# Part-of-12 stages of the second MLP projection: four seven-product blocks at 0, 3, 6, 8 instead of three at 0, 4, 8

## The chip, the cores and the metric

The kernel runs on one core of a Trainium2 chip. The metric is the device time of one execution in microseconds (us). The core has a matrix engine (TensorE, PE in the rows; its weight loads are PEld), a vector engine (VectorE, DVE), a scalar engine (ScalarE, ACT), GpSimd (POOL) and a sync engine (SyncE, SP) that here only issues loads from device memory.

## What is computed

One decoder layer on 256 tokens of width 2048: three mixing branches, and behind them a squared-ReLU MLP. The change touches the last product of the MLP alone:

```
h2 = rmsnorm(x, norm2_g[l])
x = x + jnp.square(jax.nn.relu(h2 @ w_mlp_in[l])) @ w_mlp_out[l]
return rmsnorm(x, final_g)
```

`w_mlp_out` is 8192 x 2048 in float32. The kernel keeps float32 accuracy by splitting every operand into a high part `hi` (rounded to the matrix engine's fast float32 format) and a remainder `lo`, and by running three matmuls, hi·hi, lo·hi and hi·lo, for each product.

## The kernel before

**Parts.** The 8192 hidden columns are done in three parts of 12, 12 and 8 blocks of 256 (`PARTS`). For each part the kernel first computes the hidden activations (stage m1, `do_m1`, `run_W`), then multiplies them with the matching rows of `w_mlp_out` in two halves `h` of 1024 output columns (stage m2s, `do_m2s`, `run_seven`), and adds the result to `x2`. The last half of the last part goes another way (`do_m2`).

**Blocks.** A block is 256 rows of the weight by 1024 output columns, for 256 tokens. Done in the standard way it is 2 x 2 x 2 half-block products (two halves each of tokens, rows and columns), each of three matmuls of 128 x 128 by 512 columns: 24 matmuls. A seven-product block gets the same result from 7 products of sums and differences (a scheme of Strassen's kind): 21 matmuls. Before, blocks 0, 4, 8 of the parts of 12 and 0, 4 of the part of 8 are done so: 3 + 3 + 3 + 3 + 2 = 14.

**Units.** The weight comes in units of 512 KB. A standard block is two units (below: 9a is the first unit of block 9, 9b the second). For each, SP loads `raw` (line 218), ACT rounds it to `hi` and DVE forms `lo` = raw - hi (both in `conv_to`). A seven-product block has three units, a, c and e, of which e has no load: `conv_seven` makes `d` = raw(a) - raw(c) on DVE, splits `d` for unit c, and builds the sums of unit e in the second raw buffer, in place, from `d` and both raw buffers, so that both stay taken until unit e is nearly done:

```
            V.tensor_add(x[:, 0, :], d[:, 1, :], a[:, 0, :])
            V.tensor_sub(x[:, 1, :], x[:, 1, :], x[:, 0, :])
            loaded[u] = (*split_unit(u, x), b)
```

The chain of a seven-product block is therefore serial: hi and lo of a, `d`, hi and lo of `d`, `b` (ACT and DVE), two in-place steps on the second raw, hi and lo of it.

**Buffers and order.** There are four `raw` buffers (`NRAW`), used in turn, and five each for `hi` and `lo`. Every engine runs its instructions in the order in which the code issues them; `begin_unit(u, 3)` issues the loads up to unit u + 5 and the conversions up to unit u + 3, then what `later` has put off (evacuations), then the matmuls of unit u. A load waits on SP until its raw buffer is free, that is until the unit four loads earlier has been converted.

**Accumulators.** `run_seven` holds all eight PSUM banks: `top` and `bot` (two banks each, the two token halves) and four side banks `p1`, `p5`, `p6`, `p7` for products that several outputs share. The side banks are read two slots after the last seven-product block (`ev_shared`, four DVE additions behind two ACT copies), `top` and `bot` at the end (`ev`, DVE instructions `m2r<-top`, `m2r<-bot`). The next stage's `top` takes the same two banks. In the code `m2r<-top` is issued inside the last unit, behind the conversions up to three units ahead: in the first half of a part that is behind a, c and e of the next stage's block 0.

**Forms.** The sums of activations that a seven-product block needs are made once per part in stage m1 (`sums`: four DVE additions, an ACT rounding and a DVE subtraction) and kept in a tile of their own for both halves.

Of the kernel before, what the change touches and what calls it, by code (L numbers as in the profile page):

```python
# [17 lines left out]
P = 128  # L18
# [18 lines left out]
PARTS = (12, 12, 8)  # L37
FIRST = [sum(PARTS[:q]) for q in range(len(PARTS) + 1)]
LAST = len(PARTS) - 1
EVERY = 4  # L40


C_G1, C_G2, C_GM, C_D, C_GLU = 0, 16, 32, 40, 48
# [53 lines left out]
def hybrid_trunk(  # L97
# [37 lines left out]
    def a4(shape, dt, name):  # L135
        return acts.tile(shape, dt, tag="a4", name=name)
# [13 lines left out]
    units, seven = [], {}  # L150

    def add_units(src, g, k0, k1):
        r = []
        for ku in range(k0, k1):
            r.append(len(units))
            units.append(src[g, ku])
        return r
# [22 lines left out]
    for q, nk in enumerate(PARTS):  # L180
        for i in range(0, nk, 2):
            g = FIRST[q] + i
            if (q, i) == (0, 0):
                ab = [add_units(w_m1, 0, 0, 3), add_units(w_m1, 1, 0, 3)]
                for j in range(2):
                    ab[j] += add_units(w_m1, j, 3, 4)
                plan.append(("m1", (q, i), ab))
            else:
                plan.append(("m1", (q, i), [add_units(w_m1, g + j, 0, 4) for j in range(2)]))
        for h in range(2):  # L190
            if (q, h) == (LAST, 1):
                for c in (2, 3):
                    plan.append(("m2", (q, c), add_units(w_m2, c, FIRST[q], FIRST[q + 1])))
                continue
            us = []
            for k in range(nk):
                ku = FIRST[q] + k
                if k % EVERY == 0:
                    n = len(units)
                    units.extend((w_seven[h, ku // EVERY, 0], w_seven[h, ku // EVERY, 1], None))  # L200
                    seven.update({n: "a", n + 1: "c", n + 2: "e"})
                    us.append((n, n + 1, n + 2))
                else:
                    us.append([add_units(w_m2, 2 * h + c, ku, ku + 1)[0] for c in range(2)])
            plan.append(("m2s", (q, h), us))
# [107 lines left out]
    def later(n, f):  # L313
        late.append((slot[0] + n, f))
# [14 lines left out]
    def run_W(groups, src, at_once=False):  # L329

        steps = [(g, i) for g, (us, _) in enumerate(groups) for i in range(len(us) - 1)]
        steps += [(g, len(us) - 1) for g, (us, _) in enumerate(groups)]
        pts = {}
        for g, i in steps:
            us, evac = groups[g]
            if g not in pts:
                pts[g] = two_banks(f"mm{us[0]}")
            pt = pts[g]  # L340
            last = 4 * len(us) - 1
            hi, lo = (w.rearrange("p a (b c) -> p (a b) c", b=2) for w in begin_unit(us[i], 3))
            for nb in range(2):
                for k in range(4):
                    PE.matmul(pt[:, nb, :], lhsT=hi[:, k, nb * P:(nb + 1) * P], rhs=src.both(4 * i + k),  # L345
                              start=4 * i + k == 0, stop=False)
            for nb in range(2):
                for k in range(4):
                    PE.matmul(pt[:, nb, T:], lhsT=lo[:, k, nb * P:(nb + 1) * P], rhs=src.hi(4 * i + k),  # L349
                              start=False, stop=4 * i + k == last)  # L350
            if i == len(us) - 1:
                if at_once:
                    evac(pt)
                else:
                    later(1, lambda pt=pt, evac=evac: evac(pt))
            end_unit()

    def wide_sum(ps, name):

        t = t2k([P, 2, T], name)  # L360
        S.copy(t, ps[:, :, T:])  # L361
        V.tensor_add(t, ps[:, :, :T], t)
        return t
# [169 lines left out]
    def split2(dst, i, src):  # L533

        t = dst.pair(i)
        S.copy(t[:, :, 0, :], src)
        V.tensor_sub(t[:, :, 1, :], src, t[:, :, 0, :].bitcast(F32))
# [679 lines left out]
    def do_m1(q, i0, uss):  # L1217
        if i0 == 0:
            ffs[q] = Split(env, 2 * PARTS[q], f"ff{q}_")
            forms[q] = {}  # L1220

        def ev(ps, i):
            t = wide_sum(ps, f"relu{q}_{i}")

            def square():
                V.scalar_tensor_tensor(out=t, in0=t, scalar=0.0, in1=t, op0=ALU.max, op1=ALU.mult)
                split2(ffs[q], i, t)
                if i % EVERY == 0:
                    later(1, sums)

            def sums():

                f = s5w.tile([P, 4, P], F32, tag="gb", name=f"sums{q}_{i}", bufs=1)
                V.scalar_tensor_tensor(out=f[:, 0, :], in0=t[:, 0, P:], scalar=-1.0, in1=t[:, 1, P:],
                                       op0=ALU.mult, op1=ALU.subtract)
                V.scalar_tensor_tensor(out=f[:, 1, :], in0=f[:, 0, :], scalar=-1.0, in1=t[:, 0, :P],
                                       op0=ALU.mult, op1=ALU.subtract)
                V.tensor_sub(f[:, 2, :], t[:, 0, :P], t[:, 0, P:])
                V.tensor_sub(f[:, 3, :], t[:, 1, :P], f[:, 1, :])
                fs = forms[q][i] = a4([P, 4, 2, P], F32R, f"form{q}_{i}")  # L1240
                S.copy(fs[:, :, 0, :], f)
                V.tensor_sub(fs[:, :, 1, :], f, fs[:, :, 0, :].bitcast(F32))

            later(1, square)

        groups = [(us, lambda ps, i=i0 + j: ev(ps, i)) for j, us in enumerate(uss)]
        if (q, i0) == (0, 0):
            run_W(groups, xs2)
        else:
            for j, g in enumerate(groups):  # L1250
                run_W([g], xs2, at_once=i0 + j == PARTS[q] - 1)
# [96 lines left out]
def _tiles(w):  # L1348

    k, n = w.shape  # L1350
    return np.ascontiguousarray(w.reshape(k // 256, 2, P, n // 512, 512).transpose(3, 0, 2, 1, 4))
# [9 lines left out]
def _cols(v):  # L1361
    return v.reshape(-1, P).T


def _layout(x, norm1_g, w_in, b_gate, gm_norm_g, gm_w_s, gm_b_s, s5_lambda_re, s5_lambda_im, s5_log_dt,
            s5_b_re, s5_b_im, s5_c_re, s5_c_im, s5_d, s5_w_glu, s5_b_glu, w_branch, w_out, norm2_g,
            w_mlp_in, w_mlp_out, final_g):
    a = {}
    a["x"] = x.reshape(T, D)
    a["xT"] = x.reshape(T, 4, 4, P).transpose(1, 3, 2, 0)  # L1370
    a["w_in"] = _tiles(w_in[0])
    a["w_wide"] = _tiles_T(np.concatenate([w_in[0][:, c:c + MIX] for c in (0, 3 * MIX, 4 * MIX)], axis=1))
    a["w_br"] = np.stack([_tiles(w_branch[0, n]) for n in range(3)])
    a["w_out"] = _tiles(w_out[0])
    a["w_glu"] = _tiles(s5_w_glu[0])
    a["w_m1"] = _tiles_T(w_mlp_in[0])
    a["w_m2"] = _tiles(w_mlp_out[0])

    b = a["w_m2"].reshape(2, 2, -1, P, 2, 512)[:, :, ::EVERY]
    a["w_seven"] = np.stack([np.stack([b[:, r, :, :, 0], b[:, 1 - r, :, :, 1]], axis=3) for r in range(2)],  # L1380
                            axis=2)
    a["cols"] = np.concatenate([_cols(norm1_g[0]), _cols(norm2_g[0]), _cols(gm_norm_g[0]),
                                _cols(s5_d[0]), _cols(s5_b_glu[0])], axis=1)
    a["b_gate"] = b_gate[0]
    a["final_g"] = final_g
    a["gm_ws"] = gm_w_s[0].transpose(2, 0, 1)
    a["gm_bs"] = gm_b_s[0]

    def states(v):
        return v.reshape(NPAIR, P).T  # L1390

    par = np.empty((P, 3, NPAIR), np.float32)
    par[:, 0] = states(s5_lambda_re[0])
    par[:, 1] = states(s5_lambda_im[0])
    par[:, 2] = states(np.broadcast_to(s5_log_dt[0][:, None], (64, 64)))
    a["s5_par"] = par
    b = np.zeros((4, 2, 16, 8, 2, 2, 64), np.float32)
    c = np.zeros((2, 64, 8, 2, 4, 2, 16), np.float32)
    for ri, (bb, cc) in enumerate(((s5_b_re, s5_c_re), (s5_b_im, s5_c_im))):
        bb = bb[0].reshape(8, 4, 2, 64, 16)  # L1400
        cc = cc[0].reshape(8, 4, 2, 16, 64)
        for r in range(2):
            b[:, r, :, :, ri, r, :] = bb[:, :, r].transpose(1, 3, 0, 2)
            c[r, :, :, ri, :, r, :] = cc[:, :, r].transpose(3, 0, 1, 2)
    a["s5_b"] = b.reshape(P, 8, 2 * P)
    a["s5_c"] = c.reshape(P, 8, 2, 4, 32)
    return {n: np.ascontiguousarray(v) for n, v in a.items()}
# [15 lines left out]
```

## Time and profile before

| | |
|---|---|
| median of 3 runs | 1533.29 us (1532.86 to 1533.46) |
| the profiled execution | 1534.34 us |
| its span on the core | 1532.4 us |
| PE busy | 1521.0 us, 99% |
| DVE busy | 1183.3 us, 77% |
| ACT busy | 783.2 us, 51% |
| the four m2s stages of the parts of 12 | 63.38, 63.36, 63.38 and 63.36 us |

The page gives the busy time of each engine over the span, the chain of work that ended last, and the costliest groups of instructions. A matmul's row shows about 0.39 us although the next one starts 0.23 us later, since they are pipelined; so stages are read by starts, not by busy time. Instructions of DVE and ACT start up to 0.1 us before the row of the one ahead of them ends.

### The profile page before, as it was taken

Reading aid. Unit: us, or ns where it says so; the run is one execution under the profiler, and the core shown is the slowest. Engines: PE = TensorE matmul, PEld = TensorE weight load, DVE = VectorE, ACT = ScalarE, POOL = GpSimd, SP = SyncE. Lnnn points to the kernel's source line nnn. Section 1 sums busy time; section 2 is a strip of 40 time slices with the busy share of each in tenths; the row PEclk is TensorE's granted clock in tenths of the full one; section 3 lists DMA queues with packets and bytes.
Section 4 is the critical chain, followed back from the end, with each engine's and each line's share of the span. In section 5 each row is a group of like instructions: output and inputs, shape, how many; then the busy total and the mean of one; then the engine's idle time right before and its main releaser. Section 6 shows DMA issues by size and latency. Waiting matters only on the chain.

```text
span 1532.4 us, 20783 instructions
## 1 busy us (share of the span) xinstructions
PE 1521.0 (99%) x7906; PEld 1291.8 (84%) x7906; DVE 1183.3 (77%) x1588; ACT 783.2 (51%) x994; POOL 12.2 (1%) x21
## 2 busy tenths in 40 slices
PE   9999999999999999999999999999999999999997
PEld 9988888887887887898888888888888888888886
DVE  6996988999998999967655666786766678776675
ACT  7445768455555554555445444545444454544452
POOL 0000000000000000000000000000000000000000
PEclk9999999999999999999999999999999999999999
DMA  9664555555555656555665555656556466655554
GB/s 353 210 195 140 183 191 164 184 189 193 191 199 187 203 188 220 180 185 189 214 222 180 188 185 163 219 185 212 196 192 193 154 207 202 222 191 186 198 179 151
DMA packets 85507, 298.18 MB, mean 195 GB/s; under 512 B 9632, under 2 KB 10656, under 8 KB 85408
## 3 DMA queue, kind: packets, MB, share of 16 engines
q1 hardware_dynamic: 79200, 285.25, 56.2%
q10 hardware_dynamic: 6208, 11.61, 2.4%
q8 instruction: 62, 1.02, 0.3%
q14 instruction: 37, 0.30, 0.1%
HBM read 294.73 MB, written 2.10 MB: 194 GB/s over the span
## 4 chain that ended last, share of the span: by engine, by line
PE 95%; DVE 2%; DMA 1%; ACT 1%; issue 1%; SPq 0%; POOLq 0%; POOL 0%; DVEq 0%; ACTq 0%
PE mm L345 20%; PE mm L410 13%; PE mm L411 13%; PE mm L413 13%; PE mm L349 10%; PE top L436 9%; PE bot L436 8%; PE p L436 3%; PE mm L379 1%; PE mm L387 1%; PE mm L380 1%; DMA raw<-in_w_m 1%; DVE lo L91 1%; PE pb L779 1%; PE py L879 1%
## 5 line engine op out<-in xcount | busy, mean ns | idle before, releaser
L91 DVE TENSOR_TENSOR lo<-raw,hi 128x1024 fp32r<-128x1024 f32 (+1 forms) x537 | 645.8, 1219 | 169.9 <-ACT hi L241 142.9
L241 ACT CAST hi<-raw 128x1024 fp32r<-128x1024 f32 (+1 forms) x509 | 526.1, 1049 | 285.8 <-PE mm L411 113.7
L345 PE MATMUL mm<-xz,hi 128*128 128x512 f32 x1024 | 256.5, 392 | 0.0
L345 PEld LDWEIGHTS mm<-xz,hi 128*128 128x128 f32 x1024 | 184.3, 189 | 33.1
L410 PE MATMUL mm<-hi,xs 128*128 128x512 f32 x512 | 201.4, 393 | 0.0
L411 PE MATMUL mm<-hi,xs 128*128 128x512 f32 x512 | 199.6, 390 | 0.0
L349 PEld LDWEIGHTS mm<-xz,lo 128*128 128x128 f32 x1024 | 139.7, 190 | 10.0
L349 PE MATMUL mm<-xz,lo 128*128 128x256 f32 x1024 | 142.8, 282 | 0.0
L413 PE MATMUL mm<-lo,xs 128*128 128x512 f32 x512 | 136.9, 389 | 0.0
L410 PEld LDWEIGHTS mm<-hi,xs 128*128 128x128 f32 x512 | 96.1, 188 | 23.5 <-issue 4.1
L413 PEld LDWEIGHTS mm<-lo,xs 128*128 128x128 f32 x512 | 96.1, 188 | 20.2
L411 PEld LDWEIGHTS mm<-hi,xs 128*128 128x128 f32 x512 | 96.2, 188 | 19.4
L436 PE MATMUL bot<-hi,ff 128*128 128x512 f32 x364 | 98.6, 389 | 0.0
L345 PE MATMUL mm<-xs,hi 128*128 128x512 f32 x384 | 96.9, 394 | 0.0
L436 PE MATMUL top<-hi,ff 128*128 128x512 f32 x336 | 89.8, 389 | 0.0
L345 PEld LDWEIGHTS mm<-xs,hi 128*128 128x128 f32 x384 | 69.1, 189 | 13.6 <-issue 0.7
L436 PEld LDWEIGHTS bot<-hi,ff 128*128 128x128 f32 x364 | 68.3, 188 | 14.3
L91 DVE TENSOR_TENSOR rt<-bu,cs 128x1024 f32<-128x1024 f32 x64 | 76.5, 1218 | 0.3
L436 PEld LDWEIGHTS top<-hi,ff 128*128 128x128 f32 x336 | 63.1, 188 | 13.2
L436 PE MATMUL bot<-lo,ff 128*128 128x512 f32 x182 | 57.2, 389 | 0.0
L91 DVE TENSOR_TENSOR relu<-mm,relu 128x512 f32<-128x512 f32 x32 | 22.1, 690 | 44.6 <-ACT relu L361 44.6
L349 PEld LDWEIGHTS mm<-xs,lo 128*128 128x128 f32 x384 | 52.4, 190 | 3.8
(292 smaller groups left out, 2056.5 us busy)
## 6 DMA issues: line engine op xcount, KB each, us to landing
raw<-in_w_m SPq DMA_DIRECT2D x228, 512.0 KB, 4.3
raw<-in_w_in SPq DMA_DIRECT2D x143, 512.0 KB, 4.1
raw<-in_w_wide SPq DMA_DIRECT2D x48, 512.0 KB, 3.9
raw<-in_w_br SPq DMA_DIRECT2D x48, 512.0 KB, 4.4
raw<-in_w_out SPq DMA_DIRECT2D x32, 512.0 KB, 4.3
raw<-in_w_seven SPq DMA_DIRECT2D x28, 512.0 KB, 4.6
x<-in_x ACTq DMA_DIRECT2D x8, 512.0 KB, 6.5
raw<-in_w_glu SPq DMA_DIRECT2D x8, 512.0 KB, 4.5
```

The source lines that it names most:

```text
L91: return fn(*a, **kw)
L241: S.copy(hi[:, k, :], raw[:, k, :])
L345: PE.matmul(pt[:, nb, :], lhsT=hi[:, k, nb * P:(nb + 1) * P], rhs=src.both(4 * i + k), start=4 * i + k == 0, stop=False)
L349: PE.matmul(pt[:, nb, T:], lhsT=lo[:, k, nb * P:(nb + 1) * P], rhs=src.hi(4 * i + k), start=False, stop=4 * i + k == last)
L379: PE.matmul(po, lhsT=wh, rhs=src.hi(kt), start=kt == 0 and nb % 2 == 0, stop=False)
L380: PE.matmul(po, lhsT=wh, rhs=src.lo(kt), start=False, stop=False)
L387: PE.matmul(po, lhsT=lo[:, k, nb * P:(nb + 1) * P], rhs=src.hi(kt), start=False, stop=kt == 2 * nk - 1 and nb % 2 == 1)
L410: PE.matmul(ps[tt], lhsT=xh, rhs=hi[:, k, :], start=kt == 0, stop=False)
L411: PE.matmul(ps[tt], lhsT=xl, rhs=hi[:, k, :], start=False, stop=False)
L413: PE.matmul(ps[tt], lhsT=xh, rhs=lo[:, k, :], start=False, stop=kt == 2 * nk - 1)
L436: PE.matmul(bank[b], lhsT=x, rhs=w, start=b not in begun, stop=left[b] == 0)
L779: PE.matmul(pbs[h][i][:, ri * T:(ri + 1) * T], lhsT=s5bs[h // 4][r, h % 4, ri * P:(ri + 1) * P], rhs=s5x[h // 4][r, h % 4, :], start=True, ...
```

## The change

The table `SEVEN` gives the positions of the seven-product blocks by the size of the part; `BLOCKS` lists them over all 32 blocks. Parts of 12 get four such blocks, at 0, 3, 6 and 8; the part of 8 keeps 0 and 4. That is 4 x 4 + 2 = 18. The array `w_seven` holds the same rows of the weight as before and those of the new blocks, so the bytes that are loaded don't change, only the array from which some come.

```diff
-EVERY = 4
+SEVEN = {12: (0, 3, 6, 8), 8: (0, 4)}
+BLOCKS = [f + k for f, n in zip(FIRST, PARTS) for k in SEVEN[n]]
...
-                if k % EVERY == 0:
+                if k in SEVEN[nk]:
                     n = len(units)
-                    units.extend((w_seven[h, ku // EVERY, 0], w_seven[h, ku // EVERY, 1], None))
+                    units.extend((*(w_seven[h, BLOCKS.index(ku), e] for e in range(2)), None))
...
-                if i % EVERY == 0:
+                if i in SEVEN[PARTS[q]]:
                     later(1, sums)
...
-    b = a["w_m2"].reshape(2, 2, -1, P, 2, 512)[:, :, ::EVERY]
+    b = a["w_m2"].reshape(2, 2, -1, P, 2, 512)[:, :, BLOCKS]
```

SP's order of loads in the first half of the first part, before, from the a unit of block 4 to that of block 8 (`in_w_seven` marks the two loads of a seven-product block):

```order
L218 DMA raw337_8789<-in_w_seven 128x1024
L218 DMA raw338_8807<-in_w_seven 128x1024
L218 DMA raw340_8841<-in_w_m2 128x1024
L218 DMA raw341_8861<-in_w_m2 128x1024
L218 DMA raw342_8884<-in_w_m2 128x1024
L218 DMA raw343_8893<-in_w_m2 128x1024
L218 DMA raw344_8908<-in_w_m2 128x1024
L218 DMA raw345_8923<-in_w_m2 128x1024
L218 DMA raw346_8941<-in_w_seven 128x1024
L218 DMA raw347_8959<-in_w_seven 128x1024
```

and now, from the a unit of block 3 to the second load of block 8:

```order
L219 DMA raw335_8764<-in_w_seven 128x1024
L219 DMA raw336_8779<-in_w_seven 128x1024
L219 DMA raw338_8813<-in_w_m2 128x1024
L219 DMA raw339_8833<-in_w_m2 128x1024
L219 DMA raw340_8856<-in_w_m2 128x1024
L219 DMA raw341_8865<-in_w_m2 128x1024
L219 DMA raw342_8880<-in_w_seven 128x1024
L219 DMA raw343_8895<-in_w_seven 128x1024
L219 DMA raw345_8929<-in_w_m2 128x1024
L219 DMA raw346_8949<-in_w_m2 128x1024
L219 DMA raw347_8972<-in_w_seven 128x1024
L219 DMA raw348_8981<-in_w_seven 128x1024
```

Between two pairs of `in_w_seven` stood six loads; now there are four between blocks 3 and 6 and two between blocks 6 and 8. With four buffers in turn, the two loads of block 8 take the buffers of the two loads of block 6.

DVE's order from the last conversion of block 4 to `d` of block 8, before (the number behind `lo` is the unit; `d` has the number of unit c):

```order
L91 TENSOR_TENSOR lo339_8869<-raw338_8807,hi339_8868 128x1024
L91 TENSOR_TENSOR lo340_8887<-raw340_8841,hi340_8886 128x1024
L91 TENSOR_TENSOR lo341_8896<-raw341_8861,hi341_8895 128x1024
L91 TENSOR_TENSOR lo342_8911<-raw342_8884,hi342_8910 128x1024
L91 TENSOR_TENSOR lo343_8926<-raw343_8893,hi343_8925 128x1024
L91 TENSOR_TENSOR lo344_8944<-raw344_8908,hi344_8943 128x1024
L91 TENSOR_TENSOR lo345_8962<-raw345_8923,hi345_8961 128x1024
L91 TENSOR_TENSOR lo346_8978<-raw346_8941,hi346_8977 128x1024
L91 TENSOR_TENSOR d347_8995<-raw346_8941,raw347_8959 128x1024
```

and now, from the in-place steps of block 6 to `d` of block 8:

```order
L92 TENSOR_TENSOR raw343_8895<-d343_8931,raw342_8880 128x512
L92 TENSOR_TENSOR raw343_8895<-raw343_8895 128x512
L92 TENSOR_TENSOR lo344_8957<-raw343_8895,hi344_8956 128x1024
L92 TENSOR_TENSOR lo345_8975<-raw345_8929,hi345_8974 128x1024
L92 TENSOR_TENSOR lo346_8984<-raw346_8949,hi346_8983 128x1024
L92 TENSOR_TENSOR lo347_8997<-raw347_8972,hi347_8996 128x1024
L92 TENSOR_TENSOR d348_9011<-raw347_8972,raw348_8981 128x1024
```

Two standard units instead of six stand between the end of one chain and the next block's a unit.

## Rows read from the trace of the kernel before

**Rows 1.** The page: span, and busy time of PE.

```profile
span 1532.4 us, 20783 instructions
PE 1521.0 (99%) x7906; PEld 1291.8 (84%) x7906; DVE 1183.3 (77%) x1588; ACT 783.2 (51%) x994; POOL 12.2 (1%) x21
```

**Rows 2.** Busy by stretch, first part's two m2s stages: PE, PEld, DVE, ACT, POOL, clock, DMA.

```profile
959.79:1023.17 63.38, 63.38 (x281) 52.36 (x280) 47.97 (x48) 33.04 (x37) 0.00 (x0) 1.00 0.62 206
1023.17:1086.53 63.36, 63.36 (x280) 52.36 (x279) 45.94 (x46) 30.00 (x32) 0.00 (x0) 1.00 0.64 215
```

**Rows 3.** Timeline of PE, first half: start, us, engine, line, operation, tiles, shape.

```profile
975.49 0.39 PE L436 MATMUL top<-hi,ff 128*128 128x512 f32 x1
...
980.93 0.39 PE L436 MATMUL p<-hi,ff 128*128 128x512 f32 x1
...
984.82 0.39 PE L436 MATMUL p<-lo,form 128*128 128x512 f32 x1
...
985.73 0.39 PE L436 MATMUL top<-hi,ff 128*128 128x512 f32 x1
...
1005.93 0.39 PE L436 MATMUL p<-lo,form 128*128 128x512 f32 x1
...
1025.21 0.39 PE L436 MATMUL top<-hi,form 128*128 128x512 f32 x1
```

**Rows 4.** Timeline of ACT, DVE and SP over block 4's conversion chain.

```profile
972.48 1.05 ACT L251 CAST hi<-raw 128x1024 fp32r<-128x1024 f32 x1 [0.85 <-PE bot L436]
...
974.71 1.22 DVE L91 TENSOR_TENSOR d<-raw,raw 128x1024 f32<-128x1024 f32 x1
...
979.61 0.33 SPq L218 DMA_DIRECT2D raw<-in_w_m  x1
...
981.46 4.83 DVE L91 TENSOR_TENSOR lo<-raw,hi 128x1024 fp32r<-128x1024 f32 x4 [1.19 <-ACT hi L251]
...
982.71 0.33 SPq L218 DMA_DIRECT2D raw<-in_w_m  x1
```

**Rows 5.** The timeline just ahead of that: block 3's two units being converted.

```profile
965.46 4.63 DVE L91 TENSOR_TENSOR lo<-raw,hi 128x1024 fp32r<-128x1024 f32 x4 [0.26 <-ACT hi L241]
...
970.58 1.05 ACT L241 CAST hi<-raw 128x1024 fp32r<-128x1024 f32 x1 [1.79 <-DMA raw<-in_w_m]
```

**Rows 6.** DMA issues over both stages of the first part, median us to landing.

```profile
raw<-in_w_m SPq DMA_DIRECT2D x40, 512.0 KB, 4.2
raw<-in_w_seven SPq DMA_DIRECT2D x10, 512.0 KB, 4.9
```

**Rows 7.** DMA issues, the single load issued at 1025.76.

```profile
raw<-in_w_m SPq DMA_DIRECT2D x1, 512.0 KB, 3.5
```

**Rows 8.** DMA issues, the single loads issued at 983.85 and at 984.99.

```profile
raw<-in_w_m SPq DMA_DIRECT2D x1, 512.0 KB, 4.6
...
raw<-in_w_m SPq DMA_DIRECT2D x1, 512.0 KB, 5.2
```

**Rows 9.** Timeline of DVE and ACT, end of the first half, start of the second.

```profile
1000.52 3.63 DVE L91 TENSOR_TENSOR lo<-raw,hi 128x1024 fp32r<-128x1024 f32 x3 [1.20 <-ACT hi L251]
...
1010.43 2.35 DVE L91 TENSOR_TENSOR lo<-raw,hi 128x1024 fp32r<-128x1024 f32 x2
...
1012.04 1.05 ACT L251 CAST hi<-raw 128x1024 fp32r<-128x1024 f32 x1 [1.66 <-PE bot L436]
1013.13 1.22 DVE L91 TENSOR_TENSOR lo<-raw,hi 128x1024 fp32r<-128x1024 f32 x1 [0.35 <-ACT hi L251]
...
1022.17 1.22 DVE L91 TENSOR_TENSOR m2r<-top,m2r 128x1024 f32<-128x1024 f32 x1
```

**Rows 10.** Timeline, second half: DVE's conversions of 2a, 2b, 3a; the load of 3b.

```profile
1028.22 0.33 SPq L218 DMA_DIRECT2D raw<-in_w_m  x1
...
1029.43 3.49 DVE L91 TENSOR_TENSOR lo<-raw,hi 128x1024 fp32r<-128x1024 f32 x3
```

**Rows 11.** Instructions on the sums in stage m1: duration min/median/max, first and last start.

```profile
L91 DVE TENSOR_TENSOR form<-sums,form x3: 692/692/693, 1105.8 to 1195.1; 128x512 fp32r<-128x512 f32 x3
```

## The prediction

> **What bounds the kernel now.** I read the page first: PE is busy for 1521.0 of 1532.4 us [rows 1], so a matmul that goes away can shorten the run, and a wait put ahead of PE lengthens it. Next the busy time by stretch over the stages that change [rows 2]: in both m2s stages of the first part PE is busy for the whole stretch, 63.38 of 63.38 us; the reader is to see that PE waits for nothing there now. The second part's stages read the same. DVE has 48.0 us of work in those 63.4 and ACT 33.0, so on average neither is full. The average doesn't decide, though: what matters is how early each converted unit is ready, and that is read from the timelines of PE and of the converters.
>
> In block 4, PE starts at 980.93, reaches the matmul that needs the lo of unit e (`p<-lo,form`) at 984.82, 3.89 later, and leaves the block at 985.73 [rows 3]. That lo starts at 981.46 [rows 4] and takes 1.22, so it is there at 982.68: 2.1 us early. Block 8's e lo (start 1000.52 [rows 9], end 1001.75) is needed at 1005.93 [rows 3]: 4.2 early. These leads are what the change spends.
>
> **The saving.** A seven-product block takes PE 985.73 - 980.93 = 4.80 us, a standard block 980.93 - 975.49 = 5.44 [rows 3]. That is 0.64 us for three matmuls. Four blocks change over (one in each of two halves of two parts): **-2.56 us**. It is the most the change can gain, and it is 0.17% of the run; 0.2%, or 3.07 us, is about what a measurement of this kernel tells from no change.
>
> **Edits at nothing.** The loads are as many and as large. Each part makes one more set of sums in stage m1: four small DVE additions and a 0.69 us subtraction [rows 11]; three sets do so in the part now and PE waits for none. Without that cover it would be some 2 us a part. The additional DVE and ACT work of the four blocks is not priced as busy time but through the chain below. The part of 8 is unchanged.
>
> **The chain of a seven-product block.** From `d` (974.71) to the end of the e lo (982.68) is 7.98 us [rows 4]: DVE and ACT wait for each other in turn, so it is a latency. The a unit's raw buffer comes free 4.90 after `d` starts (next load at 979.61), the other 8.00 after (982.71) [rows 4]. From the hi of a to `d` is 2.23 (972.48 to 974.71).
>
> **First half, block by block.** Block 3 starts on PE at 975.49 as now [rows 3]. Its a unit is in the place of 3a, whose lo is the last of the four that end at 965.46 + 4.63 = 970.09; its second load is in the place of 3b, which lands by 970.58 [rows 5]. So `d` starts at 970.6 and the e lo ends at 978.6; PE needs it at 975.49 + 3.89 = 979.4. It is 0.8 early: no wait.
>
> Block 6 is loaded into the buffers of 4a and 4b, which are converted right behind that e lo, at DVE's spacing of 1.14. So its a load is issued 8.00 + 1.14 = 9.14 after `d` of block 3, as second of a burst of three; loads in that place of a burst landed after 4.6, the next after 5.2 [rows 8]. `d` of block 6 then starts 9.14 + 4.6 + 2.23 = 16.0 after `d` of block 3, at 986.6, and the e lo is there at 994.6; PE, at block 6 from 975.49 + 4.80 + 10.88 = 991.17, needs it at 995.06. Still 0.5 early.
>
> Block 8 takes the buffers of block 6. Its second load can't be issued before block 6's chain is over, 8.00 after that `d`, and its own `d` needs it landed. **That landing is the term the trace doesn't show in place**: a load issued alone. The lowest near row is 3.5 [rows 7]; the median of the `w_seven` loads, most of them in bursts, is 4.9 [rows 6]. I take 3.8, near the lone load, and keep both ends. So `d` of block 8 starts at 986.6 + 8.0 + 3.8 = 998.4 and the e lo ends at 1006.4. PE, at block 8 from 991.17 + 4.80 + 5.44 = 1001.41, needs it at 1005.3. **Wait: 1.1 us** (0.8 to 2.2).
>
> By the Trainium skill (DMA: Bandwidth & Descriptors, Anatomy of one DMA) a DMA takes about 2 us plus its bytes at 436 GB/s, fitted there for loads issued by GpSimd; for 512 KB that is 3.2 us, an estimate, and with it in this one place the net sum below would come to +4.6. The trace has 3.5 at its lowest near row and 4.2 as the median.
>
> **The turn to the second half.** Now PE is level with the e lo of block 8, where it was 4.2 behind. In the trace `m2r<-top` ends at 1022.17 + 1.22 = 1023.39, 21.64 after the e lo of block 8 (1001.75) [rows 9]: it stands on DVE behind the four additions on the side banks and the whole chain of the next block 0. PE goes from the need of that e lo to the first matmul that writes the new `top`, which needs those banks read, in 1025.21 - 1005.93 = 19.28 [rows 3]. Before, the 4.2 covered this difference. Part of the 21.64 is a cast that waited for PE to free a hi buffer (1.66 idle at 1012.04 [rows 9]), which a PE further on doesn't cause: without it the lo at 1013.13 follows the one that ends at 1012.78, 0.4 earlier. So the wait is 21.2 - 19.3 = **1.9 us** (to 2.4).
>
> **Second half.** Time from the end of `m2r<-top`, J. The lo of 3a, now block 3's a, ends at 1029.43 + 3.49 = 1032.92 [rows 10]; `d` starts there, J + 9.45 (its second load, issued at 1028.22, is there by then at 4.0). The e lo ends at J + 17.43. PE has 2.76 left of block 0, two blocks and 3.89: 17.53. It is 0.1 early. From there to block 8 the converters need 16.0 + 8.0 + 3.8 = 27.8, PE only 2 x 4.80 + 3 x 5.44 = 25.92. **Wait: 27.8 - 25.9 - 0.1 = 1.8 us** in blocks 6 and 8 (1.5 to 2.9).
>
> **The turn to stage m1.** `m2r<-top` stands here behind the third m1 unit. That one loads into 11a's buffer, free 9.9 after the e lo of block 8 (1010.43 + 1.2 against 1001.75 [rows 9]); landing 3.8, hi and lo 2.3 and the read 1.2 make 17.2. PE comes to the new accumulator after 0.91 + 16.32 = 17.23. **Wait: 0** (to 1.1).
>
> **Sum.** Each part: 1.1 + 1.9 + 1.8 = 4.8 us of waits. Two parts: 9.6; less 2.56: **+7.0 us**. The profiled execution took 1534.34 us, 1.05 over the median of the runs, which is the yardstick: 1533.3 + 7.0 = **1540.3 us**. With the lone load at 3.5 it is +5.8, with 4.4 about +11.5.
>
> **Rivals.**
> *The bursts don't queue.* Landing sets it all: if the loads of a burst also came in 3.5 [rows 7], as now only lone ones do, `d` of block 6 would start 14.9 after that of block 3, and 3 to 8 would take 26.4 against PE's 25.9. Then block 8's unit is 0.3 early in the first half, the turn costs 1.6, the second half 0.4: 2.0 a part, +1.4 in all, **1534.7**, not slower by more than can be told. It turns into a gain once landings and lead together hide another 0.7 us a part, at most to **1530.7**. For it: the four units of block 8's surroundings are only 0.5 to 2 us short, and DVE has 15 us idle in each stage [rows 2]. Against it: the 4.6 and 5.2 of [rows 8] are loads in just that place.
> *Loads from `w_seven` stay slow alone.* At 4.9 [rows 6] the waits are 2.2 + 2.4 + 2.9 + 1.1 = 8.6 a part: +14.6, **1547.9**. Against it: those rows are mostly bursts.
> *The change does not save what it says.* A seven-product block could need PE as long as a standard one if its waits were inside the 4.80; they are not, as PE is busy throughout [rows 2].
>
> **How the numbers follow.** Forecast, slower by 4 to 12 us: 0.72. Bursts that don't queue, or a longer lead: 0.19, of which 0.02 I leave for a gain over 0.2%, which the full saving doesn't reach. Slow lone loads: 0.09. The forecast's own range is 1538 to 1545; 8 in 10 are held from 1534.5 to 1546.5. Slower by over 0.2% (above 1536.4): 0.81; within 0.2%: 0.17; faster: 0.02.
>
> **What would show it.** In the changed kernel's timeline: PE waits of 1 to 2 us in the first half inside block 8, ended by a lo; about 2 us ahead of the first `top` matmul of the second half, ended by `m2r<-top`; 1.5 to 2 us in the second half's blocks 6 and 8; the same again in the second part; none in the m1 stages, none in block 3. A saving of 0.64 per added block between waits. The forecast is wrong if the second load of block 8 lands before 997 on the time axis of the rows, or if PE's busy time still fills the stages.

## The result, and the profile after

The changed kernel takes 1541.75 us (median of 5 runs, 1539.96 to 1543.09); beside it the kernel before takes 1533.01 us (5 runs, 1532.39 to 1533.46). The ratio is 1.0056, with an interval of 1.0045 to 1.0066: slower by 8.7 us. The profiled execution took 1540.96 us.

The page's head, which answers to [rows 1]:

```profile
span 1539.1 us, 20811 instructions
...
PE 1521.3 (99%) x7894; PEld 1287.9 (84%) x7894; DVE 1203.4 (78%) x1618; ACT 788.9 (51%) x1004; POOL 12.3 (1%) x21
```

The change does what it says: 12 matmuls fewer than before. Yet PE's busy time hasn't fallen, because a matmul's row also grows when the one behind it is held up (0.50 us in rows below, where [rows 3] have 0.39). The stages tell more. Busy time by stretch, the four m2s stages of the parts of 12, as in [rows 2] (stretch, us; PE, PEld, DVE, ACT, POOL; clock; DMA share; GB/s):

```profile
959.30:1024.53 65.23, 63.75 (x279) 51.49 (x277) 49.46 (x51) 31.81 (x36) 0.00 (x0) 1.00 0.57 192
1024.53:1090.83 66.30, 63.78 (x277) 51.39 (x276) 52.04 (x53) 33.26 (x35) 0.00 (x0) 1.00 0.62 204
1224.91:1288.93 64.02, 63.30 (x279) 51.66 (x278) 49.54 (x51) 31.92 (x36) 0.00 (x0) 1.00 0.59 197
1288.93:1354.89 65.96, 63.60 (x277) 51.47 (x276) 51.96 (x53) 32.93 (x35) 0.00 (x0) 1.00 0.62 205
```

PE no longer fills the stretches: 65.23 us hold 63.75 us of busy time where 63.38 held 63.38 before. The two stages of the first part take 131.53 us together and those of the second 129.98; before they took 126.75 in each part. That is 4.78 + 3.23 = 8.01 us more. The first and second m1 stages behind them last 134.07 and 89.36 us, against 134.05 and 89.36. So the time was lost inside the four stages and nowhere else. (The spans of the two profiled executions differ by 6.7 us and not by 8.0, because that of before was 0.49 us longer ahead of these stages and 0.82 longer behind the last m2s stage.)

PE's waits between 900 and 1500 us (engine, line, what was waited for: us in total, times, longest). For the kernel before, this view has no row at all:

```profile
PE top L437 <- DVE m2r L92: 3.3, 2, 1.7
PE p L437 <- DVE lo L92: 2.6, 5, 0.5
PE p L437 <- ACT hi L252: 1.1, 4, 0.4
```

The places, in PE's timeline. In brackets stands the idle time and what ended it; since the row ahead is drawn 0.16 us too long and the next matmul starts another 0.11 late, a wait read from start to start is 0.27 us longer than its bracket. Waits of about 0.1 us show no bracket; one of 0.10 belongs to the wait at 995.35, so that this one is 0.9 us:

```profile
995.35 0.50 PE L437 MATMUL p<-lo,form 128*128 128x512 f32 x1 [0.53 <-DVE lo L92]
...
1005.91 0.73 PE L437 MATMUL p<-hi,form 128*128 128x512 f32 x2 [0.43 <-ACT hi L252]
...
1007.17 0.50 PE L437 MATMUL p<-lo,form 128*128 128x512 f32 x1 [0.53 <-DVE lo L92]
...
1028.41 0.74 PE L437 MATMUL top<-hi,form 128*128 128x512 f32 x2 [1.68 <-DVE m2r L92]
...
1072.21 0.74 PE L437 MATMUL p<-hi,form 128*128 128x512 f32 x2 [0.31 <-ACT hi L252]
1073.47 0.50 PE L437 MATMUL p<-lo,form 128*128 128x512 f32 x1 [0.52 <-DVE lo L92]
...
1292.77 0.73 PE L437 MATMUL top<-hi,form 128*128 128x512 f32 x2 [1.64 <-DVE m2r L92]
```

995.35 is block 6 of the first half, 1005.91 and 1007.17 block 8, 1028.41 the first matmul on `top` in the second half, 1072.21 and 1073.47 that half's block 8. In [rows 3] the matmuls in these places (1005.93 `p<-lo,form`, 1025.21 `top<-hi,form`) waited for nothing.

What the converters did meanwhile, in the timeline of DVE and SP over the first half (answers to [rows 4, 5, 9]), and `d` in the second half:

```profile
970.18 1.23 DVE L92 TENSOR_TENSOR d<-raw,raw 128x1024 f32<-128x1024 f32 x1 [0.34 <-DMA raw<-in_w_seven]
...
979.34 1.46 SPq L219 DMA_DIRECT2D raw<-in_w_seven  x2
...
987.31 1.22 DVE L92 TENSOR_TENSOR d<-raw,raw 128x1024 f32<-128x1024 f32 x1
...
992.21 3.44 SPq L219 DMA_DIRECT2D raw<-in_w_seven  x2
...
994.07 4.63 DVE L92 TENSOR_TENSOR lo<-raw,hi 128x1024 fp32r<-128x1024 f32 x4 [1.19 <-PE top L437]
...
999.15 1.23 DVE L92 TENSOR_TENSOR d<-raw,raw 128x1024 f32<-128x1024 f32 x1 [0.45 <-DMA raw<-in_w_seven]
...
1005.89 4.63 DVE L92 TENSOR_TENSOR lo<-raw,hi 128x1024 fp32r<-128x1024 f32 x4 [1.19 <-ACT hi L252]
...
1027.14 1.22 DVE L92 TENSOR_TENSOR m2r<-top,m2r 128x1024 f32<-128x1024 f32 x1
...
1037.73 1.22 DVE L92 TENSOR_TENSOR d<-raw,raw 128x1024 f32<-128x1024 f32 x1
...
1053.80 1.22 DVE L92 TENSOR_TENSOR d<-raw,raw 128x1024 f32<-128x1024 f32 x1
...
1065.45 1.23 DVE L92 TENSOR_TENSOR d<-raw,raw 128x1024 f32<-128x1024 f32 x1 [0.26 <-DMA raw<-in_w_seven]
```

The e lo of block 6 starts at 994.07 and takes 1.23, and PE goes on at 995.35; that of block 8 ends at 1007.12, and PE goes on at 1007.17. `m2r<-top` ends at 1028.36, and PE goes on at 1028.41. The `d` of block 8 starts with the landing of its own second load, which is the second of the two issued from 992.21 on (its 0.33 end the row at 995.65, so it starts at 995.32).

Landing of single loads (DMA issues; the last number is us from issue to landing), as [rows 7, 8]: block 6's first load, issued at 979.34 in a burst, and its second at 980.47; block 8's second load, issued at 995.32, and in the second half at 1061.81; block 6's first load in the second half (1046.88) and in the second part (1245.10):

```profile
raw<-in_w_seven SPq DMA_DIRECT2D x1, 512.0 KB, 5.7
...
raw<-in_w_seven SPq DMA_DIRECT2D x1, 512.0 KB, 5.8
...
raw<-in_w_seven SPq DMA_DIRECT2D x1, 512.0 KB, 3.8
...
raw<-in_w_seven SPq DMA_DIRECT2D x1, 512.0 KB, 3.6
...
raw<-in_w_seven SPq DMA_DIRECT2D x1, 512.0 KB, 4.6
...
raw<-in_w_seven SPq DMA_DIRECT2D x1, 512.0 KB, 4.2
```

### The profile page after: what moved, and what is told of

Same layout as the page of the kernel before. It is cut to its first block, busy times and chain, and to the rows that moved or that the text cites. A ratio compares the mean times of both kernels' runs of the same rounds, so it can differ in the third digit from the quotient of the medians.

```text
span 1539.1 us, 20811 instructions
## 1 busy us (share of the span) xinstructions
PE 1521.3 (99%) x7894; PEld 1287.9 (84%) x7894; DVE 1203.4 (78%) x1618; ACT 788.9 (51%) x1004; POOL 12.3 (1%) x21
## 4 chain that ended last, share of the span: by engine, by line
PE 91%; DVE 4%; ACT 2%; DMA 2%; issue 1%; SPq 0%; POOLq 0%; DVEq 0%; POOL 0%; ACTq 0%
PE mm L346 20%; PE mm L411 13%; PE mm L412 13%; PE mm L414 13%; PE mm L350 10%; PE top L437 7%; PE bot L437 6%; PE p L437 3%; DVE lo L92 2%; PE mm L380 1%; PE mm L388 1%; PE mm L381 1%; DMA raw<-in_w_m 1%; ACT hi L252 1%; ACT hi L242 1%
## 5 line engine op out<-in xcount | busy, mean ns | idle before, releaser
L242 ACT CAST hi<-raw 128x1024 fp32r<-128x1024 f32 (+1 forms) x501 | 516.7, 1049 | 254.6 <-PE mm L412 115.1
L437 PE MATMUL bot<-hi,ff 128*128 128x512 f32 x340 | 92.5, 390 | 0.0
L437 PE MATMUL top<-hi,ff 128*128 128x512 f32 x304 | 81.3, 389 | 0.0
L437 PEld LDWEIGHTS bot<-hi,ff 128*128 128x128 f32 x340 | 63.8, 188 | 13.2
L252 ACT CAST hi<-raw 128x1024 fp32r<-128x1024 f32 x36 | 37.8, 1050 | 64.0 <-DVE raw L92 38.9
L437 PEld LDWEIGHTS top<-hi,ff 128*128 128x128 f32 x304 | 57.1, 188 | 12.0
```

Source lines behind the costliest of these rows:

```text
L242: S.copy(hi[:, k, :], raw[:, k, :])
L252: S.copy(hi, raw)
L437: PE.matmul(bank[b], lhsT=x, rhs=w, start=b not in begun, stop=left[b] == 0)
```

## The experiments

The theory: with four raw buffers a chain can't begin before the chain ahead has released its buffers and a load has landed in them, so four serial chains in a half come later than PE needs them. The rivals: DVE and ACT are too slow for four chains whatever the buffers; or one place, the turn or the landing of one load, makes most of the time. Like the prediction's sum, the theory took the waits as terms that can be taken away one by one. Each diff is against the changed kernel. All ratios are against the kernel before, run on the same chip. In the readings, "a part" is the two m2s stages of a part of 12, from matmul start to matmul start.

### A fifth raw buffer

```diff
-NACT = 32
+NACT = 31
...
-NRAW = 4
+NRAW = 5
```

`NACT` pays for the memory of `NRAW`: one activation buffer fewer.

> The changed kernel with five raw buffers in place of four (one activation buffer less, 31, makes the room). Theory (block 8's loads wait for block 6's raw buffers, everything else follows): no PE wait of over 0.3 us in the m2s stages, each part's two halves together about 125.5 us (126.75 before, less 2 x 0.64), the run about 2.6 us faster than the kernel before. Rival (the conversion chain on ACT and DVE is itself too slow for this spacing): the waits stay, 130 to 131.5 us a part, the run 6 to 9 us slower than before.

1530.02 us (10 runs, 1529.91 to 1530.42) against 1532.56; ratio 0.9983 (0.9974 to 0.9992). Busy time by stretch, both parts:

```profile
958.70:1084.17 125.47, 125.47 (x554) 103.62 (x553) 101.16 (x103) 64.69 (x72) 0.00 (x0) 1.00 0.63 213
1218.22:1343.69 125.47, 125.47 (x554) 103.61 (x553) 101.08 (x103) 64.68 (x72) 0.00 (x0) 1.00 0.63 213
```

PE fills both parts and the view of its waits is empty again. A part takes 125.47, which is 126.75 less two times 0.64: the saving came whole, 2.56 us by the stages and 2.54 by the medians. DVE has the same work as in the changed kernel (49.46 + 52.04 = 101.5 us there, 101.16 here), so it was not DVE's amount of work that cost the time. The `d` of blocks 3, 6 and 8 show what the buffer did:

```profile
968.92 1.22 DVE L92 TENSOR_TENSOR d<-raw,raw 128x1024 f32<-128x1024 f32 x1
...
983.25 1.23 DVE L92 TENSOR_TENSOR d<-raw,raw 128x1024 f32<-128x1024 f32 x1 [0.32 <-DMA raw<-in_w_seven]
...
994.56 1.22 DVE L92 TENSOR_TENSOR d<-raw,raw 128x1024 f32<-128x1024 f32 x1
```

From block 6's to block 8's it is 11.31 us instead of 11.84, and from block 3's to block 6's 14.33 instead of 17.13. PE's work in the same two stretches is 4.80 + 5.44 = 10.24 and 4.80 + 2 x 5.44 = 15.68 us. So in this half the buffer gave most between blocks 3 and 6, where the converters now gain 1.35 us of lead and no longer lose 1.45; between 6 and 8 they still lose 1.07, and the lead covers that. This version beats both kernels.

### The fifth buffer with the old positions

The same two lines, and the positions of before:

```diff
-SEVEN = {12: (0, 3, 6, 8), 8: (0, 4)}
+SEVEN = {12: (0, 4, 8), 8: (0, 4)}
```

> Control: the same five raw and 31 activation buffers with the positions 0, 4, 8 of the kernel before. Theory: PE waits for nothing in these stages already, so 126.75 us a part and no change of the run beyond 0.2%. If buffers helped by something else (the front of the kernel, the last stage), it would show here as a gain.

1532.53 us (10 runs, 1532.36 to 1533.03) against 1532.56; ratio 1.0000 (0.9991 to 1.0009). A part takes 126.75, as before, with no wait. So the buffer by itself is worth nothing where three blocks are done with seven products, and the 2.54 us of the run above belong to the added blocks.

### One activation buffer fewer, alone

```diff
-NACT = 32
+NACT = 31
```

> Control for the five-buffer run: the changed kernel with four raw buffers and 31 activation buffers. Theory: the same waits as the changed kernel, 129 to 132 us a part, 5 to 10 us slower than before. Rival (the smaller activation pool changed something by itself): it would move toward the five-buffer run's 125.5 us a part.

1540.65 us (4 runs, 1540.31 to 1542.02) against 1532.5; ratio 1.0051 (1.0034 to 1.0068). The interval overlaps that of the changed kernel, PE's waits are the same three kinds, and the parts take 132.19 and 131.07 us, the first just over what was expected. So in the run with the fifth buffer it was the buffer that helped, not the one taken away.

### Three blocks, at 0, 6 and 8

```diff
-SEVEN = {12: (0, 3, 6, 8), 8: (0, 4)}
+SEVEN = {12: (0, 6, 8), 8: (0, 4)}
```

The close pair 6, 8 is left, without block 3 ahead of it: as many seven-product blocks as before.

> Three seven-product blocks as before, but at 0, 6, 8: the dense pair alone. Theory (the lead of four us at block 6 pays for one short spacing, it takes two in a row, 0-3-6-8, to use it up): no wait in blocks 6 and 8, at most 0.5 us at the turn; 126.75 to 127.8 us a part; the run within 0.2% of before. Rival (two standard units between two chains always cost a wait): 1.2 to 1.5 us in block 8 and 1.9 at the turn in each part, about 130 us a part, the run 5 to 7 us slower.

1533.08 us (10 runs, 1532.64 to 1533.89) against 1532.56; ratio 1.0004 (0.9994 to 1.0013). The parts take 127.26 and 126.87. In the first part PE waits once, at the turn:

```profile
1024.49 0.73 PE L437 MATMUL top<-hi,form 128*128 128x512 f32 x2 [0.21 <-DVE m2r L92]
```

So the close pair alone is almost covered by the lead that PE leaves the converters up to block 6; of about 5 us of waits a part some 0.5 and 0.1 are left. It needs block 3 ahead of the pair to use the lead up.

### `m2r<-top` issued one unit earlier

```diff
-                w1 = begin_unit(u[1], 3)
+                w1 = begin_unit(u[1], 2)
                 std(u[1], k, 1, 0, w1)
                 evac[1](0, top)
+                conv_to(u[1] + 3)
```

The read of `top` then stands on DVE ahead of the last unit of the next block 0's chain instead of behind it.

> The changed kernel with the read of top issued on DVE ahead of the conversion of the next unit e, not behind it. Theory (the turn's wait is DVE's order): the wait of 1.9 us ahead of the first top matmul of the second half falls under 0.5; the e unit of the next block 0 and the read of bot come later for it, which gives back some: in all 1 to 3 us less than the changed kernel. The waits inside blocks 6 and 8 stay in the first half. Rival (PE waits there since all conversions are late, whatever their order): the same 1.9 us wait stands there or one matmul group further, and the run is as slow as the changed kernel.

1541.45 us (4 runs, 1540.31 to 1542.06) against 1532.56; ratio 1.0057 (1.0042 to 1.0072): no better than the changed kernel. PE's timeline, from the turn into the second half:

```profile
1028.28 0.73 PE L437 MATMUL bot<-hi,ff 128*128 128x512 f32 x2 [0.61 <-DVE m2r L92]
...
1044.50 0.50 PE L437 MATMUL p<-lo,form 128*128 128x512 f32 x1 [0.49 <-DVE lo L92]
...
1060.72 0.50 PE L437 MATMUL p<-lo,form 128*128 128x512 f32 x1 [0.26 <-DVE lo L92]
```

The edit did its part: PE waits 0.9 us at the turn instead of 1.95, and for `bot` instead of `top`. But block 3 now waits 0.8 us and block 6 0.5, where the changed kernel has none and 0.2. What was gained at the turn is lost in the next blocks. The rival's time came, though its 1.9 us did not stay in one place. The theory's gain did not come, and with it falls the view that each wait is a term for itself. What the rows show fits another reading: once PE is level with the converters, the total is set by how long their chains take from end to end, and removing a wait moves it, as long as no chain gets shorter.

### Block 8's gating load in two halves

The second load of each seven-product block is issued as two loads of 256 KB:

```diff
-            w = 2 // parts
+            w = 2 // (2 if seven.get(u) == "c" else parts)
```

> The changed kernel with the load of unit c issued as two of 256 KB; d needs only the first of them. Theory (the landing of block 8's second load is on the path): d of block 8 starts earlier by what the half lands sooner, 0.3 to 1.5 us, so the waits in block 8 shrink by as much in each half, those at the turn by little; the run 1 to 4 us less than the changed kernel, still slower than before. Rival (the landing is hidden, the chain alone sets it): as slow as the changed kernel.

1539.3 us (4 runs, 1538.43 to 1539.61) against 1532.5; ratio 1.0042 (1.0027 to 1.0057). DMA issues over the first part (the count, KB each, median us to landing):

```profile
raw<-in_w_m SPq DMA_DIRECT2D x34, 512.0 KB, 4.4
raw<-in_w_seven SPq DMA_DIRECT2D x7, 512.0 KB, 4.5
raw<-in_w_seven SPq DMA_DIRECT2D x14, 256.0 KB, 3.4
```

The timeline of DVE, `d` of blocks 6 and 8 of the first half:

```profile
985.69 1.22 DVE L92 TENSOR_TENSOR d<-raw,raw 128x1024 f32<-128x1024 f32 x1
...
997.06 1.22 DVE L92 TENSOR_TENSOR d<-raw,raw 128x1024 f32<-128x1024 f32 x1
```

From block 6's `d` to block 8's it is 11.37 us instead of 11.84, and the wait in block 8 falls from 1.5 to 0.8 us in the first half and from 1.4 to 1.1 in the second. Two other things changed that the edit does not aim at. Block 6's first load, still whole, landed earlier than in the changed kernel (4.8 us against 5.65), and block 6 doesn't wait in the first half. And at the turn of the first part, where little was to change, PE waits 3.1 us and not 1.95; there the first load of the next block 0, issued whole at 1008.51, took 7.4 us. The landings of the two loads, and the wait:

```profile
raw<-in_w_seven SPq DMA_DIRECT2D x1, 512.0 KB, 4.8
...
raw<-in_w_seven SPq DMA_DIRECT2D x1, 512.0 KB, 7.4
...
1027.48 0.74 PE L437 MATMUL top<-hi,form 128*128 128x512 f32 x2 [2.79 <-DVE m2r L92]
```

By the medians the run gives back about 2 of the 8.7 us, though the intervals of the two ratios overlap, so that the size is uncertain, and how much of it the halved load gave and how much the other landings is not separated. The parts took 130.64 and 129.48 in the profile, 1.4 us less in all than those of the changed kernel. The landing is on the path of block 8, but a quicker one is not enough: with the fifth buffer, block 8's `d` no longer waits for it.

### The fifth buffer, and three blocks in the part of 8 too

With the fifth buffer, 19 seven-product blocks:

```diff
-SEVEN = {12: (0, 3, 6, 8), 8: (0, 4)}
+SEVEN = {12: (0, 3, 6, 8), 8: (0, 3, 5)}
```

> Five raw and 31 activation buffers, and a third seven-product block in the part of 8, at 0, 3, 5 in place of 0, 4: 19 blocks. Theory (with five buffers only PE's matmuls count): the last part's first half takes 42.27 - 0.64 = 41.63 us, the parts of 12 125.5 us as with 18, no wait; 3.2 us faster than before, 0.6 more than with 18. Rival (the short spacing of 3 to 5 costs a wait of 1 us or more there): as with 18, or slower.

1530.14 us (10 runs, 1529.69 to 1531.06) against 1532.5; ratio 0.9984 (0.9975 to 0.9993): nothing beyond the first experiment. The stage of the part of 8 takes 42.64 us where 42.27 - 0.64 = 41.63 were to be had. So the theory missed and the rival of this run is right. A wait in block 5, 1.0 us from start to start, takes the rest:

```profile
1463.76 0.50 PE L437 MATMUL p<-lo,form 128*128 128x512 f32 x1 [0.52 <-DVE lo L92]
```

### The fifth buffer, and five blocks in the parts of 12

```diff
-SEVEN = {12: (0, 3, 6, 8), 8: (0, 4)}
+SEVEN = {12: (0, 2, 4, 6, 8), 8: (0, 4)}
```

This asks what bounds the work once buffers don't.

> Five raw and 31 activation buffers, five seven-product blocks in the parts of 12, at 0, 2, 4, 6, 8 (22 in all). Theory (now the chain on ACT and DVE is the next bound): a seven-product and a standard block take the converters 8.9 + 2.3 = 11.1 us or more and PE 4.80 + 5.44 = 10.24, so each block from 2 on waits about 0.9 us, and block 2 of each half more, since its chain begins late: 4 to 10 us of waits a part against 6 x 0.64 us saved; slower than before by 5 to 17 us. Rival (loads alone were the limit, and five buffers are enough at any spacing): no waits, 5.1 us faster than before.

1551.16 us (4 runs, 1550.95 to 1551.26) against 1532.5; ratio 1.0120 (1.0105 to 1.0135). The timeline of DVE and PE in the second half, `d` of blocks 4, 6 and 8 and the end of the wait in each on PE:

```profile
1047.26 1.22 DVE L92 TENSOR_TENSOR d<-raw,raw 128x1024 f32<-128x1024 f32 x1
...
1055.27 0.50 PE L437 MATMUL p<-lo,form 128*128 128x512 f32 x1 [0.53 <-DVE lo L92]
...
1058.54 1.22 DVE L92 TENSOR_TENSOR d<-raw,raw 128x1024 f32<-128x1024 f32 x1
...
1066.56 0.50 PE L437 MATMUL p<-lo,form 128*128 128x512 f32 x1 [0.53 <-DVE lo L92]
...
1069.83 1.22 DVE L92 TENSOR_TENSOR d<-raw,raw 128x1024 f32<-128x1024 f32 x1
...
1077.85 0.50 PE L437 MATMUL p<-lo,form 128*128 128x512 f32 x1 [0.52 <-DVE lo L92]
```

No `d` waits for a load. They come every 11.28 us, and PE has only 4.80 + 5.44 = 10.24 us of work in that time: a wait of 1.05 in every pair of blocks, and the parts take 136.18 and 135.81. The mechanism was as expected and the cost just over the end of its range. The rival of this run, no waits, is out; the first of the rivals listed ahead of the experiments, ACT and DVE too slow, is right here. At every second block, the chain and the conversions of one standard block take longer than PE's work, and what they wait for is each other (ACT and DVE in turn), not a buffer or a load.

## Why the prediction was right, step by step

The forecast was 1540.3 us, slower, in 1534.5 to 1546.5; it is 1541.75. The reasons held as well, except for the size of one term and for the view that each wait stands alone. The waits in us, from start to start:

| term | predicted, a part | first part | second part |
|---|---|---|---|
| first half, block 6 | 0 | 0.9 | 0 |
| first half, block 8 | 1.1 | 1.5 | 1.3 |
| turn to the second half | 1.9 | 1.95 | 1.9 |
| second half, blocks 6 and 8 | 1.8 | 1.6 | 1.3 |
| turn to m1 | 0 | 0 | 0 |
| sum | 4.8 | 6.0 | 4.5 |

By the stages, each against the 125.47 us without a wait, the waits are 6.06 and 4.51, 10.6 in all where 9.6 was forecast. Less 2.56, that is the 8.01 us above against +7.0. That the total came so near is in part luck: the first part is 1.3 us over its sum and the second 0.3 under it, and the runs of the changed kernel differ by 3.1 us.

**The saving.** Right: 2.56 us in the first experiment's stages, and 2.54 in its medians.

**The chain and the buffers.** Right to a tenth. Block 6's first load is issued 9.16 us after block 3's `d` (979.34 against 970.18; worked out: 9.14). Its hi starts as soon as it has landed, and its `d` 2.22 behind that (worked out: 2.23). Block 8's `d` follows block 6's after 11.84 and 11.65 us (worked out: 8.0 + 3.8 = 11.8). In the second half block 3's `d` comes 9.37 after the end of `m2r<-top` (worked out: 9.45), and block 6's 16.07 after that (16.0).

**The lone landing.** The prediction took 3.8 as nearest to a lone load; measured: 3.8 and 3.6 in the first part, 3.8 and 3.5 in the second. The estimate worked out there from the Trainium skill (DMA: Bandwidth & Descriptors, Anatomy of one DMA) is 3.2 us, shorter than any of them; the measurement decides.

**The burst's landing: the term that was mis-sized.** "Still 0.5 early" for block 6 of the first half rested on 4.6 for a load in the second place of a burst. It took 5.65 there (5.7 in the row above). That is 1.05 more than taken, and with it block 6 waits 0.9 us and block 8 another 0.4 more than forecast. The same load took 4.6 in the second half and 4.2 in the second part, where block 6 waits 0.2 and 0. So the mean was near and the spread was left out: a margin of 0.5 us was called "no wait" against landings that differ by 1.4 from place to place.

**The turn.** Right in size: from the end of block 8's e lo to the end of `m2r<-top` it is 21.24 us (1007.12 to 1028.36; worked out: 21.2), and the wait is 1.95. Not right as a term that stands alone: with `top` read earlier, the wait came back in blocks 3 and 6.

**The rivals.** Bursts that don't queue are out: in the four stages, the loads issued 1.1 us behind another took 4.1 to 6.2. Lone loads at 4.9 are out: block 8's took 3.5 to 3.8. That the change would not save what it says is out by the first experiment. That DVE and ACT bound the work is out for four blocks, where with the fifth buffer PE waits for nothing, and shown for five.

Not tried was whether the wider spread of the times comes from those landings: the five runs of the changed kernel differ by 3.1 us, the ten with the fifth buffer by 0.5, and the two parts of one execution by 1.55.

## What to carry to other kernels

Where a faster method costs a longer preparation, compare the rates first: the saving comes only while the preparation of one block, its buffers' release and the load into them included, takes no longer than the work it feeds, or while the lead lasts. When the lead is gone, don't cure the waits one by one, since the next one takes over; look for what lengthens the chain from end to end, here one buffer of 512 KB, which turned +8.7 us into -2.5. The Trainium skill (Perfetto Trace Analysis, Optimization Strategy) says that bubbles that repeat on the engine that should be saturated can mean too few buffers for the next tile; the runs here agree, and add the limit: with five such blocks the waits return at 1.05 us a pair, and there it is not the buffers.

## What was not expected of the hardware

A 512 KB load's landing depends on its company more than on the array that it comes from: single ones from `w_seven` took 3.6 and 3.8 us in the changed kernel, one from `w_m2` 3.5 [rows 7], and those issued 1.1 us behind another took 4.1 to 6.2 in the four stages, with 5.65 and 4.25 for the same load of the program in two parts of one execution (5.7 and 4.2 in the rows above). Half the bytes did not halve it: the loads of 256 KB had a median of 3.4 us, those of 512 KB beside them 4.4 and 4.5. And PE's waits of up to 1.95 us did not lower its granted clock, which stays at 1.00 in all four stretches, the level of 2.4 GHz.
